# State-space taps of the second network's odd layer: shifted copies kept in DRAM, loads moved to GpSimd's queue, small products reordered

## The chip, the cores and the metric

The program runs on one core of one Trainium2 chip. The metric is the device time of one execution in microseconds (us), lower is better. Engines are named as in the profile: PE (TensorE matmul), PEld (TensorE weight load), DVE (VectorE), ACT (ScalarE), POOL (GpSimd), SP (SyncE, which here only issues transfers). All transfers, whoever issues them, are run by the core's 16 DMA engines.

## The reference

The program is a chain of two small networks on 256 tokens of width 2048. The part that matters here is the odd layer of the second network: a linear projection, a diagonal state-space model ("s5") on 128 groups of 16 channels, a gated linear unit, an output projection, and around it cross-attention to a memory and a squared-ReLU feed-forward layer.

```
def s5_mixer(u, lam_re, lam_im, log_dt, b_re, b_im, c_re, c_im, d_skip, w_glu, b_glu):
    ...
    lam_bar = jnp.exp(lam * dt)
    b_bar = ((lam_bar - 1.0) / lam)[..., None] * lax.complex(b_re.astype(f32), b_im.astype(f32))
    c_mat = lax.complex(c_re.astype(f32), c_im.astype(f32))
    ...
    def chunk_step(state, u_c):
        bu = jnp.einsum('bcgi,gpi->bcgp', u_c.astype(jnp.complex64), b_bar)
        bu = bu.at[:, 0].add(lam_bar * state)
        _, states = lax.associative_scan(combine, (a_elem, bu), axis=1)
        y = jnp.einsum('bcgp,gip->bcgi', states, c_mat).real
        return states[:, -1], y
    ...
    z = jax.nn.gelu(y)
    out = z * jax.nn.sigmoid(z @ w_glu.astype(f32) + b_glu.astype(f32))
    return out.astype(u.dtype)
```

## The kernel before

The kernel is written against a framework that takes the operations in program order, gives each engine's instructions an order by a timeline of its own, and adds the waits. A change in the program can therefore move instructions that it does not mention.

The dense layers read each weight tile (512 KB, tile `wraw`) on SP's queue, copy its high part on ACT (`wh`, L308), take the low part on DVE (`wl`, L309), and multiply both on PE. `dense_p` (L392, L393) holds the weight as the stationary operand, and `mm_t` (L344 to L346) and `mm_n` (L350 to L352) are two other forms. `wraw` has 3 buffers here, `wh` and `wl` 2 each and one more inside some stages.

The state-space layer is turned into products of small matrices, in 8 blocks of 16 groups, in two halves of the program.

The first half, `s5_gen` with `s5_block`, is a generator. It runs in the background of the first feed-forward layer (`ffn(0)`, about 1840 to 2600 us), a step at each tick. For each block it makes three tables and stores them in DRAM on ACT's queue (`store`, L269): `GD` (input to state, 1 MB per block), `HD` (state to output, 1 MB), and `KD` (the taps of the direct path). The taps come from 16 products `pk` (L1833, operands `bd` and `H`), 8 of them with the stationary operand in each half; each writes 32 of the 128 output columns of the array, and `o` picks which by `g % 4`. `KD` holds for each group and channel a row of 240 numbers: 112 zeros (`zpad`, written once) and 128 taps.

The second half, `odd`, runs after it (about 2600 to 3050 us):

- `v_gen` (L1888 on) loads `GD` as tile `gts`, multiplies it with the input `U` (L1898), transposes (L1905) and carries the states (`V`).
- beside it and behind it, `memkv` (L1606 on) makes keys and values of the memory from the weights `xattn_wkv` and the tile `mm`; its products are the L344 to L346 and L350 to L352 whose operand is `mhl`.
- then a loop over the 8 blocks, two at a time (`B`): DVE carries the states and copies them to one of two tiles `Xb` (L1976); the tile `tts` (1 MB) gets the taps, 8 shifted windows of `KD`, one transfer per shift (L1979); the tile `hts` gets `HD` (L1981); PE multiplies `U` with `tts` (L1986, 32 columns each) and `Xb` with `hts` (L1990, 64 columns each), both into `py`; ACT copies (`ys`, L1992), PE transposes (L1997), DVE adds (`zs`, L2001). Each two blocks give four tiles of the gated unit's input, and `glu_gen` steps through its weights (`s5_w_glu`, in the trace `s_w_glu`) in between.

`gts`, `tts` and `hts` share one tag with 3 buffers, so the load of a tile waits until the products of an earlier one have been issued and done. All these loads stand on SP's queue among the weight loads, in one order:

```
1978  for t in range(8):
1979      nc.sync.dma_start(tt[16 * t:16 * t + 16], KD[16 * blk:16 * blk + 16, :, 112 - 16 * t:240 - 16 * t].rearrange("g j x -> j g x"))
1981  nc.sync.dma_start(ht.rearrange("p a b c -> p (a b c)"), HD[blk])
```

A row of the first transfer is 128 numbers, 512 B, and one block has 2048 such rows; a row of the second is 2048 numbers, 8 KB.

POOL has little to do: among others it fills `zpad` and `Xb` with zeros, copies `pr`, and raises to the power of minus a half for the norms (`pow_mhalf`, L465), once near the start of `ffn(0)` and once in `odd`.

Of the kernel before, what the change touches and what calls it, by code (L numbers as in the profile page):

```python
# [10 lines left out]
F32 = mybir.dt.float32  # L11
# [11 lines left out]
HD = 128  # L23
# [190 lines left out]
class Prog:  # L214
# [1490 lines left out]
    def s5_gen(self, p, dr):  # L1705

        nc, a = self.nc, self.a
        GD, HD, KD = dr
        eng = nc.gpsimd
        f = lambda v: v.rearrange("p a b -> p (a b)")  # L1710
        lam = p.tile([128, 3, 64], F32, name="lam")
# [56 lines left out]
            nc.gpsimd.tensor_copy(pr[:, :, i], pw[:, :, 7 - i])  # L1768
        z = p.tile([128, 16, 112], F32, name="zpad", tag="G")
        nc.gpsimd.memset(z, 0.0)  # L1770
        self.store(KD[:, :, :112], z)
        yield
        for blk in range(8):
            yield from self.s5_block(p, dr, pw, pr, fb, blk)
# [5 lines left out]

    def s5_block(self, p, dr, pw, pr, fb, blk):
        nc, a = self.nc, self.a
        GD, HD, KD = dr
        keep = self.tc.keep_in_program_order
        gs = slice(blk * 8, blk * 8 + 8)
        bc = self.s5bc.pop(0)
# [34 lines left out]
        for i, (x, y, op) in enumerate(((0, 2, ALU.add), (2, 0, ALU.subtract))):  # L1821
            for g in range(0, 8, GS):
                c = slice(g, g + GS)
# [3 lines left out]
                yield  # L1827

        pk = self.sm((4, 128))
        for g in range(8):  # L1830
            o = pk[32 * (g % 4):32 * (g % 4) + 32, g // 4]
            for i in range(2):
                nc.tensor.matmul(o, bd[:, i, g].rearrange("p a b -> p (a b)"), H[:, i, g, :8].rearrange("p a b -> p (a b)"), start=i == 0, stop=i == 1)  # L1833
        self.store(HD[blk].rearrange("p (r g x) -> p r g x", r=2, g=8), H[:, :, :, 1:].rearrange("p r g t i -> p r g (t i)"))
        kc = p.tile([128, 2, 128], F32, name="kc", bufs=2)
        nc.scalar.copy(kc, pk[:, :2])
        for s in range(2):
            g0 = 16 * blk + 8 * s
            self.store(KD[g0:g0 + 8].rearrange("g j x -> (g j) x")[:, 112:], kc[:, s])
        yield  # L1840

        G = p.tile([128, 2, 8, 8, 16], F32, name="G", tag="G")
# [21 lines left out]
    def odd(self, x, uT, dr, kv, st, st_out):  # L1864

        nc, a = self.nc, self.a
        GD, HD, KD, UD = dr
        with self.pool("ohz") as hp, ExitStack() as es:
            up = es.enter_context(self.pool("ou"))
            U = up.tile([128, 128, 32], F32, name="U")  # L1870
# [16 lines left out]
            def v_gen():  # L1887

                for blk in range(8):
                    gt = sp.tile([128, 8, 2, 128], F32, name="gts", tag="st", bufs=3)  # L1890
                    nc.sync.dma_start(gt.rearrange("p a b c -> p (a b c)"), GD[blk])

                    pv = self.sm((2, 2, 128))
                    for g in range(8):
                        q = slice(32 * (g % 4), 32 * (g % 4) + 32)
                        for h in range(2):
                            hs = slice(64 * h, 64 * h + 64)
                            nc.tensor.matmul(pv[q, g // 4, :, hs], Ug(2 * (8 * blk + g) + h), gt[:, g, :, hs], start=True, stop=True)  # L1898
                    vs, ct = (lambda v: (v[:, 0], v[:, 1]))(up.tile([128, 8, 8, 16], F32, name="ys", bufs=2).rearrange("p (z i r) a b -> p z i r (a b)", z=2, i=2))
                    nc.scalar.copy(vs, pv)  # L1900
                    yield
                    tp = self.sm((2, 2, 4, 32))
                    for i in range(2):
                        for r in range(2):
                            nc.tensor.transpose(tp[:, r, i].rearrange("p a b -> p (a b)"), vs[:, i, r], self.cst("ident"))  # L1905
                    for r in range(2):
                        nc.scalar.copy(V[:, :, r, 8 * blk:8 * blk + 8], tp[:, r].rearrange("p i q c -> p c (i q)"))
                    carry(0, 1, 2, 16, L8, 8 * blk, ct.rearrange("p i r x -> p (i r x)"))
                    carry(1, 3, 4, 8, L16, 8 * blk, ct.rearrange("p i r x -> p (i r x)"))
                    yield  # L1910
# [54 lines left out]
            for B in range(4):  # L1965
                ys = up.tile([128, 8, 8, 16], F32, name="ys", bufs=2)
                for blk in (2 * B, 2 * B + 1):
# [7 lines left out]
                        for i in range(2):  # L1975
                            nc.vector.tensor_copy(xb[r, i, :, h, 1:], V[r, :31, i, gs].rearrange("p c g -> p g c"))  # L1976
                    tt = sp.tile([128, 16, 128], F32, name="tts", tag="st", bufs=3)
                    for t in range(8):
                        nc.sync.dma_start(tt[16 * t:16 * t + 16], KD[16 * blk:16 * blk + 16, :, 112 - 16 * t:240 - 16 * t].rearrange("g j x -> j g x"))  # L1979
                    ht = sp.tile([128, 2, 8, 128], F32, name="hts", tag="st", bufs=3)  # L1980
                    nc.sync.dma_start(ht.rearrange("p a b c -> p (a b c)"), HD[blk])  # L1981
                    py = self.sm((4, 128))
                    for b in range(4):
                        for q in range(4):
                            g = 4 * b + q
                            nc.tensor.matmul(py[32 * q:32 * q + 32, b], Ug(16 * blk + g), tt[:, g], start=b == 0, stop=False)  # L1986
                    for g in range(8):
                        o = py[64 * (g % 2):64 * (g % 2) + 64, g // 2]
                        for i in range(2):
                            nc.tensor.matmul(o, xb[:, i, g].rearrange("p a b -> p (a b)"), ht[:, i, g], start=False, stop=(i == 1 and g >= 6))  # L1990
                    b0 = 4 * (blk % 2)
                    nc.scalar.copy(ys[:, :, b0:b0 + 4], py.rearrange("p b (t i) -> p t b i", t=8))  # L1992
                zs = up.tile([128, 4, T], F32, name="zs", tag="zs", bufs=1)
# [89 lines left out]
    def second(self, xc, st):  # L2083
# [5 lines left out]
        GD = dp.tile([8, 128, 2048], F32, name="GD")  # L2089
        HD = dp.tile([8, 128, 2048], F32, name="HD")  # L2090
        KD = dp.tile([128, 16, 240], F32, name="KD")
        self.blocks = [dp.tile([128, 32, 32], F32, name=n) for n in ("MD", "XD", "YD")]
        UD = dp.tile([D, T], F32, name="UD")
        out = self.stat()
# [4 lines left out]
        with self.wide("w3"):  # L2099
            self.xattn(0, x, kv, st, s2)  # L2100
            st = self.stat()
            with self.pool("s5p") as p:
                self.bg.append(self.s5_gen(p, (GD, HD, KD)))
                self.ffn(0, x, s2, st, RF)
        s1 = self.stat()
        kv = (self.es.enter_context(self.pool("kv1")).tile([128, 4, T], F32, name="mkT"), kv[1])
        self.odd(x, xc[:, 0], (GD, HD, KD, UD), kv, st, s1)
        s2 = self.stat()
        s3 = self.stat()
        with self.wide("w4"):  # L2110
# [65 lines left out]
```

## Time and profile before

| | |
|---|---|
| three runs | 3854.62, 3855.39, 3858.6 us, median 3855.39 |
| the profiled execution | 3850.04 us, of which the span of instructions is 3848.3 us |
| PE busy | 3654.7 us (95%), at a mean granted clock of 0.975 |
| DVE, ACT, POOL busy | 2694.8 (70%), 1680.5 (44%), 102.1 us (3%) |
| DMA | 700.74 MB, 57.1% of 16 engines on SP's queue, 2.4% on ACT's, 0.4% on POOL's |

The profiled execution is 5.35 us below the median of the runs. A window of the profile gives for a stretch of the span how long each engine was busy, the granted PE clock as a share of full speed, and the DMA share (mean busy share of the 16 engines; packets in flight overlap, so it can pass 1). The chain view follows back from the last instruction what released it, step by step.

### The profile page before, as it was taken

What the parts mean: (1) busy time and instruction counts of PE and PEld (TensorE: products, weight loads), DVE (VectorE), ACT (ScalarE), POOL (GpSimd) and SP (SyncE); (2) the same over time, 40 slices, a digit from 0 to 9 for tenths busy, and PEclk for the clock granted to TensorE, in tenths of its full rate; (3) what the DMA queues carried; (4) which work ended last, traced back from release to release, by engine and by line L of the source; (5) the groups of instructions that cost most, each with busy time, mean ns of one, the idle gap of its engine ahead of it and who ended that gap; (6) DMA issues with size and microseconds to landing.
All of it is one profiled execution on the core that took longest, in us unless ns stands there. A gap on an engine that the chain in (4) does not pass through costs nothing.

```text
span 3848.3 us, 54892 instructions
## 1 busy us (share of the span) xinstructions
PE 3654.7 (95%) x21008; PEld 3029.0 (79%) x21008; DVE 2694.8 (70%) x4732; ACT 1680.5 (44%) x2524; POOL 102.1 (3%) x138
## 2 busy tenths in 40 slices
PE   6999999989999999899999999999879999999997
PEld 2677777777678889777888888887778788888886
DVE  3568777765776878767987778786666676656565
ACT  3313233262564566425544444444325454445353
POOL 0010000001000001000000000000000000000000
PEclk8999999999999999889999999999989999999999
DMA  9745544555655544524666666668985556666664
GB/s 343 244 145 176 158 149 156 175 170 174 215 152 158 142 137 140 164 67 145 188 214 197 208 200 208 198 211 247 223 197 181 165 154 191 187 191 187 190 186 148
DMA packets 609335, 700.74 MB, mean 182 GB/s; under 512 B 52208, under 2 KB 493680, under 8 KB 605744
## 3 DMA queue, kind: packets, MB, share of 16 engines
q1 hardware_dynamic: 576304, 662.39, 57.1%
q10 hardware_dynamic: 31488, 30.64, 2.4%
q0 software_dynamic: 1280, 4.20, 0.4%
q8 instruction: 165, 2.70, 0.3%
q14 instruction: 98, 0.80, 0.1%
HBM read 672.63 MB, written 24.51 MB: 181 GB/s over the span
## 4 chain that ended last, share of the span: by engine, by line
PE 82%; DMA 9%; DVE 6%; ACT 2%; issue 1%; SPq 0%; ACTq 0%; POOL 0%; DVEq 0%; POOLq 0%
PE acc L392 33%; PE acc L393 17%; PE acc L344 4%; PE acc L345 4%; PE acc L346 4%; PE acc L350 3%; PE acc L352 3%; PE acc L351 3%; DMA wraw<-ada_w 2%; DVE wl L309 2%; PE sm L623 1%; ACT wh L308 1%; PE sm L600 1%; DMA wraw<-w_in 1%; DMA tts<-KD 1%
## 5 line engine op out<-in xcount | busy, mean ns | idle before, releaser
L308 ACT CAST wh<-wraw 128x1024 fp32r<-128x1024 f32 x994 | 1037.7, 1045 | 1486.3 <-PE acc L392 734.1
L309 DVE TENSOR_TENSOR wl<-wraw,wh 128x1024 fp32r<-128x1024 f32 x994 | 1208.5, 1217 | 643.8 <-ACT wh L308 639.6
L392 PE MATMUL acc<-hl,wh 128*128 128x512 f32 x3008 | 1060.4, 400 | 21.9 <-DVE hl L490 15.1
L393 PE MATMUL acc<-hl,wl 128*128 128x256 f32 x3008 | 827.3, 284 | 4.3 <-DVE wl L309 4.3
L392 PE MATMUL acc<-hid,wh 128*128 128x512 f32 x2048 | 709.9, 394 | 1.4 <-DVE xc L526 1.0
L392 PEld LDWEIGHTS acc<-hl,wh 128*128 128x128 f32 x3008 | 559.3, 190 | 150.4 <-DVE hl L490 11.6
L393 PEld LDWEIGHTS acc<-hl,wl 128*128 128x128 f32 x3008 | 567.9, 190 | 23.4 <-DVE wl L309 8.1
L393 PE MATMUL acc<-hid,wl 128*128 128x256 f32 x2048 | 559.8, 280 | 0.0
L392 PEld LDWEIGHTS acc<-hid,wh 128*128 128x128 f32 x2048 | 378.3, 188 | 85.6 <-issue 1.8
L393 PEld LDWEIGHTS acc<-hid,wl 128*128 128x128 f32 x2048 | 380.9, 188 | 9.0 <-issue 3.4
L571 DVE SCALAR_TENSOR_TENSOR ada_a<-wraw,sc,ada_a 128x512 f32<-128x512 f32 x360 | 253.5, 749 | 19.6 <-DMA wraw<-ada_w 18.7
L344 PE MATMUL acc<-hl,wh 128*128 128x512 f32 (+2 forms) x688 | 256.0, 376 | 7.7 <-ACT wh L308 3.8
L345 PE MATMUL acc<-hl,wh 128*128 128x512 f32 (+2 forms) x688 | 252.9, 369 | 0.0
L346 PE MATMUL acc<-hl,wl 128*128 128x512 f32 (+2 forms) x688 | 247.1, 369 | 0.0
L350 PE MATMUL acc<-wh,hl 128*128 128x512 f32 (+1 forms) x504 | 200.1, 402 | 4.0 <-ACT wh L308 2.5
L351 PE MATMUL acc<-wh,hl 128*128 128x512 f32 (+1 forms) x504 | 199.7, 396 | 0.0
L352 PE MATMUL acc<-wl,hl 128*128 128x512 f32 (+1 forms) x504 | 189.2, 395 | 4.4 <-DVE wl L309 4.4
L526 DVE TENSOR_TENSOR xc<-acc,xc 128x256 f32<-128x256 f32 x384 | 141.8, 419 | 36.7 <-PE acc L393 36.1
L344 PEld LDWEIGHTS acc<-hl,wh 128*128 128x128 f32 (+1 forms) x688 | 130.2, 190 | 37.3 <-issue 6.6
L345 PEld LDWEIGHTS acc<-hl,wh 128*128 128x128 f32 (+1 forms) x688 | 130.0, 189 | 25.2 <-issue 5.9
L346 PEld LDWEIGHTS acc<-hl,wl 128*128 128x128 f32 (+1 forms) x688 | 129.1, 189 | 23.9 <-issue 3.2
L406 ACT COPY joined<-acc 128x256 f32<-128x256 f32 x188 | 69.5, 371 | 133.1 <-PE acc L393 133.0
(588 smaller groups left out, 4950.0 us busy)
## 6 DMA issues: line engine op xcount, KB each, us to landing
wraw<-ffn_up SPq DMA_DIRECT2D x256, 512.0 KB, 3.8
wraw<-ffn_down SPq DMA_DIRECT2D x256, 512.0 KB, 3.7
wraw<-ada_w SPq DMA_DIRECT2D x192, 512.0 KB, 4.5
wraw<-w_in SPq DMA_DIRECT2D x144, 512.0 KB, 4.4
wraw<-w_out SPq DMA_DIRECT2D x64, 512.0 KB, 4.5
wraw<-even_w_in SPq DMA_DIRECT2D x54, 512.0 KB, 3.7
wraw<-even_w_out SPq DMA_DIRECT2D x32, 512.0 KB, 3.6
wraw<-xattn_wkv SPq DMA_DIRECT2D x32, 512.0 KB, 4.7
```

Of the source, the lines that this page charges most:

```text
L308: nc.scalar.copy(hi, src)
L309: self.held(nc.vector.tensor_tensor(lo, src, hi.bitcast(F32), op=ALU.subtract))
L344: nc.tensor.matmul(A, h, xh, start=(start and first), stop=False)
L345: nc.tensor.matmul(A, h, xl, start=False, stop=False)
L346: nc.tensor.matmul(A, lo, xh, start=False, stop=(stop and last))
L350: nc.tensor.matmul(A, xh, wh[:, kk, :cw], start=start, stop=False)
L351: nc.tensor.matmul(A, xl, wh[:, kk, :cw], start=False, stop=False)
L352: nc.tensor.matmul(A, xh, wl[:, kk, :cw], start=False, stop=stop)
L392: nc.tensor.matmul(A, wh[:, kk, cs], xp, start=k == 0, stop=False)
L393: nc.tensor.matmul(A[:, 1], wl[:, kk, cs], xp[:, 0], start=False, stop=k == nk - 1)
L526: nc.vector.tensor_tensor(x[:, j + i], A[:, h], x[:, j + i], op=ALU.add)
L571: nc.vector.scalar_tensor_tensor(a[:, r], w[:, kk], c, a[:, r], op0=ALU.mult, op1=ALU.add)
```

## The change

`s5_block` now writes, as soon as a block's taps are in `KD`, the 8 shifted windows to a new array `TD` in DRAM, in the layout that `tts` has in SBUF. `odd` then loads `tts` in one transfer of 128 rows of 8 KB. The stores to `KD` (`zpad`, `kc`), the writes of `TD` (64 in all) and the loads of `gts`, `tts` and `hts` are issued by POOL. The loops over the small products `pk` and `Xb` x `hts` run in another order: four (two) groups with the first of their two terms, then the same groups with the second.

```
@@ s5_gen
-        self.store(KD[:, :, :112], z)
+        nc.gpsimd.dma_start(KD[:, :, :112], z)
@@ s5_block
-        for g in range(8):
-            o = pk[32 * (g % 4):32 * (g % 4) + 32, g // 4]
-            for i in range(2):
+        for g, i in ((4 * s + q, i) for s in range(2) for i in range(2) for q in range(4)):
+                o = pk[32 * (g % 4):32 * (g % 4) + 32, g // 4]
                 nc.tensor.matmul(o, bd[:, i, g].rearrange("p a b -> p (a b)"), H[:, i, g, :8].rearrange("p a b -> p (a b)"), start=i == 0, stop=i == 1)
...
-            self.store(KD[g0:g0 + 8].rearrange("g j x -> (g j) x")[:, 112:], kc[:, s])
+            nc.gpsimd.dma_start(KD[g0:g0 + 8].rearrange("g j x -> (g j) x")[:, 112:], kc[:, s])
+
+        for t in range(8):
+            nc.gpsimd.dma_start(TD[blk, 16 * t:16 * t + 16], KD[16 * blk:16 * blk + 16, :, 112 - 16 * t:240 - 16 * t].rearrange("g j x -> j g x"))
@@ odd
-                    nc.sync.dma_start(gt.rearrange("p a b c -> p (a b c)"), GD[blk])
+                    nc.gpsimd.dma_start(gt.rearrange("p a b c -> p (a b c)"), GD[blk])
...
-                    for t in range(8):
-                        nc.sync.dma_start(tt[16 * t:16 * t + 16], KD[16 * blk:16 * blk + 16, :, 112 - 16 * t:240 - 16 * t].rearrange("g j x -> j g x"))
+                    nc.gpsimd.dma_start(tt.rearrange("p g x -> p (g x)"), TD[blk].rearrange("p g x -> p (g x)"))
...
-                    nc.sync.dma_start(ht.rearrange("p a b c -> p (a b c)"), HD[blk])
+                    nc.gpsimd.dma_start(ht.rearrange("p a b c -> p (a b c)"), HD[blk])
...
-                    for g in range(8):
+                    for g, i in ((2 * r + h, i) for r in range(4) for i in range(2) for h in range(2)):
                         o = py[64 * (g % 2):64 * (g % 2) + 64, g // 2]
-                        for i in range(2):
-                            nc.tensor.matmul(o, xb[:, i, g].rearrange("p a b -> p (a b)"), ht[:, i, g], start=False, stop=(i == 1 and g >= 6))
+                        nc.tensor.matmul(o, xb[:, i, g].rearrange("p a b -> p (a b)"), ht[:, i, g], start=False, stop=(i == 1 and g >= 6))
@@ second
+        TD = dp.tile([8, 128, 16, 128], F32, name="TD")
```

**POOL's order.** From the zeros of `zpad` in the feed-forward layer to the loads of `odd`, before:

```order
L1770 MEMSET zpad 128x1792
L1768 COPY pr<-pw 128x2x64
L465 TENSOR_TENSOR rstd_c<-rstd_c,consts 128x2
L1768 COPY pr<-pw 128x2x64 x7
L1874 MEMSET Xb_22745 128x1024
L1874 MEMSET Xb_22746 128x1024
L465 TENSOR_TENSOR rstd_c<-rstd_c,consts 128x2 x4
```

and with the change, from the eighth block's stores to the first loads of `tts` and `hts` (a transfer of `zpad` stands between the first two rows above, and seven more pairs like the first two rows here stand ahead of these):

```order
L1838 DMA KD<-kc 128x128 x2
L1841 DMA TD<-KD 256x1x128 x8
L1876 MEMSET Xb_22810 128x1024
L1876 MEMSET Xb_22811 128x1024
L1893 DMA gts<-GD 128x2048 x3
L465 TENSOR_TENSOR rstd_c<-rstd_c,consts 128x2
L1893 DMA gts<-GD 128x2048 x5
L1980 DMA tts<-TD 128x2048
L1982 DMA hts<-HD 128x2048
```

All transfers of the state-space tables but the stores of `GD` and `HD` now follow one another on POOL, with two of its small jobs (the power for the feed-forward layer's norm and that for `odd`'s) behind some of them.

**SP's order.** Among the weight loads of `memkv`, where before

```order
L1981 DMA hts<-HD 128x2048
L314 DMA wraw<-xattn_wkv 128x2x512
L1979 DMA tts<-KD 16x16x128 x2
L1606 DMA mm<-memT 128x2x256
L1979 DMA tts<-KD 16x16x128 x6
L314 DMA wraw<-xattn_wkv 128x2x512
L1981 DMA hts<-HD 128x2048
L1979 DMA tts<-KD 16x16x128 x2
```

stood in SP's queue, with the change there are only weights and the memory, up to the gated unit's:

```order
L1606 DMA mm<-memT 128x2x256
L314 DMA wraw<-xattn_wkv 128x2x512 x2
L1606 DMA mm<-memT 128x2x256
L314 DMA wraw<-xattn_wkv 128x2x512 x3
L314 DMA wraw<-s_w_glu 128x2x512 x16
L314 DMA wraw<-s_w_glu 128x4x256 x16
```

SP loses 80 transfers and keeps the rest in nearly the same order.

**PE's order** in the feed-forward layer, around a block's first run of `pk` products (`sm<-H,bd` is a `pk` product, the dense rows are L392 and L393), before:

```order
L393 MATMUL acc<-hid,wl 128x256
L1833 MATMUL sm<-H,bd 32x128
L392 MATMUL acc<-hid,wh 128x512 x2
L1833 MATMUL sm<-H,bd 32x128 x6
L393 MATMUL acc<-hid,wl 128x256 x2
```

and with the change:

```order
L393 MATMUL acc<-hid,wl 128x256
L1832 MATMUL sm<-H,bd 32x128
L392 MATMUL acc<-hid,wh 128x512 x2
L1832 MATMUL sm<-H,bd 32x128 x3
L1859 MATMUL sm<-consts,G 128x128 x3
L393 MATMUL acc<-hid,wl 128x256 x2
```

The scheduler cuts the 128 `pk` products into 36 runs between dense products before, and into 30 with the change, and a run now holds more different groups.

## Rows read from the trace of the kernel before

**Rows 1.** The page's chain that ended last, by engine and by line.

```profile
PE 82%; DMA 9%; DVE 6%; ACT 2%; issue 1%; SPq 0%; ACTq 0%; POOL 0%; DVEq 0%; POOLq 0%
```

**Rows 2.** Windows: stretch, length, busy PE, PEld, DVE, ACT, POOL, then PEclk, DMA share, GB/s.

```profile
1860.00:2590.00 730.00, 728.60 (x4319) 622.30 (x4318) 584.78 (x954) 333.36 (x420) 4.61 (x7) 1.00 0.66 204
2724.00:2785.00 61.00, 49.22 (x384) 43.07 (x382) 33.59 (x85) 21.11 (x36) 0.00 (x0) 0.89 1.02 221
2785.00:2801.00 16.00, 9.88 (x47) 7.95 (x46) 15.28 (x49) 5.16 (x6) 0.00 (x0) 0.83 0.53 165
2801.00:2821.00 20.00, 12.36 (x169) 11.12 (x169) 19.81 (x88) 4.93 (x6) 0.00 (x0) 0.76 0.88 166
2821.00:2872.00 51.00, 43.34 (x471) 39.71 (x472) 22.87 (x49) 14.65 (x16) 0.00 (x0) 0.90 1.14 236
2872.00:2896.00 24.00, 23.38 (x199) 22.65 (x198) 10.50 (x15) 8.79 (x9) 0.00 (x0) 0.95 0.40 125
```

**Rows 3.** The chain from 2724 to 2896 us: start, length, what.

```profile
2728.32 9.80 DMA wraw<-xattn_wkv
...
2751.36 6.11 DMA tts<-KD
```

**Rows 4.** PE's waits from 2724 to 2896 us: total, times, longest.

```profile
PE sm L1990 <- DVE Xb L1976: 6.1, 1, 6.1
PE sm L1986 <- DMA tts<-KD: 6.1, 1, 6.1
...
PE sm L1990 <- DMA hts<-HD: 4.6, 3, 3.4
```

**Rows 5.** DMA, 2800 to 2880 us: tenths busy and rate per 2 us, issues.

```profile
DMA  1047999999999999999999999999999999996006
GB/s 60 8 66 291 267 122 122 123 157 389 163 128 140 166 244 329 139 146 150 191 365 413 389 153 142 166 189 340 381 284 137 167 182 246 389 406 236 2 0 162
...
hts<-HD SPq DMA_DIRECT2D x6, 1024.0 KB, 9.3
tts<-KD SPq DMA_DIRECT2D x40, 128.0 KB, 10.0
```

**Rows 6.** DMA, 2724 to 2800 us: issues, size, median to landing.

```profile
tts<-KD SPq DMA_DIRECT2D x24, 128.0 KB, 6.5
```

**Rows 7.** Timeline of SP at 2813 us: start, length, what.

```profile
2812.86 9.65 SPq L1979 DMA_DIRECT2D tts<-KD  x8
```

**Rows 8.** Timeline of PE: runs of `pk` records (two per product).

```profile
1952.28 0.66 PE L1833 MATMUL sm<-H,bd 128*32 128x128 f32 x16
...
1963.18 0.41 PE L1833 MATMUL sm<-H,bd 128*32 128x128 f32 x2
...
2018.50 0.63 PE L1833 MATMUL sm<-H,bd 128*32 128x128 f32 x6
...
2527.64 1.06 PE L1833 MATMUL sm<-H,bd 128*32 128x128 f32 x20
```

**Rows 9.** Line L1833: idle time of its engine, total and times.

```profile
  issue: 10.1, 31
```

**Rows 10.** All transfers: issues, KB each, median us to landing.

```profile
HD<-H ACTq DMA_DIRECT2D x8, 1024.0 KB, 7.4
...
x<-xc POOLq DMA_DIRECT2D x16, 256.0 KB, 3.6
```

**Rows 11.** Line L946, POOL's transfers before: ns min, median, max.

```profile
L946 POOL DMA_DIRECT2D x<-xc x16: 724/724/903, 622.4 to 764.7; - x16
```

**Rows 12.** Line L314 (weight loads) from 1956 to 1966 us.

```profile
DMA to landing us min/median/max: 4.0/5.1/5.2
```

**Rows 13.** PE's waits from 1840 to 2600 us, the one on weights.

```profile
PE acc L392 <- ACT wh L308: 0.4, 1, 0.4
```

**Rows 14.** Timeline of POOL, start of the feed-forward layer.

```profile
1837.65 1.59 POOL L1770 MEMSET zpad<- 128x1792 f32 x1 [53.04 <-DVE xc L526]
...
1856.05 0.70 POOL L465 TENSOR_TENSOR rstd_c<-rstd_c,consts 128x2 f32<-128x2 f32 x1 [16.34 <-DVE rstd_c L482]
```

More of the change, by code (lines that the diff above doesn't have):

```diff
@@ L1707, in s5_gen @@
         nc, a = self.nc, self.a
-        GD, HD, KD = dr
+        GD, HD, KD, TD = dr
         eng = nc.gpsimd
@@ L1782, in s5_block @@
         nc, a = self.nc, self.a
-        GD, HD, KD = dr
+        GD, HD, KD, TD = dr
         keep = self.tc.keep_in_program_order
@@ L1866, in odd @@
         nc, a = self.nc, self.a
-        GD, HD, KD, UD = dr
+        GD, HD, _, TD, UD = dr
         with self.pool("ohz") as hp, ExitStack() as es:
@@ L2102, in second @@
             with self.pool("s5p") as p:
-                self.bg.append(self.s5_gen(p, (GD, HD, KD)))
+                self.bg.append(self.s5_gen(p, (GD, HD, KD, TD)))
                 self.ffn(0, x, s2, st, RF)
@@ L2106, in second @@
         kv = (self.es.enter_context(self.pool("kv1")).tile([128, 4, T], F32, name="mkT"), kv[1])
-        self.odd(x, xc[:, 0], (GD, HD, KD, UD), kv, st, s1)
+        self.odd(x, xc[:, 0], (GD, HD, KD, TD, UD), kv, st, s1)
         s2 = self.stat()
```

## The prediction, made before the changed kernel ran

> **What bounds the kernel now.** I read the chain first: 82% of it is PE, and 9% is DMA [rows 1], so somewhere transfers set the pace. The windows say where [rows 2]. In the feed-forward layer (1860 to 2590) PE is busy 728.60 of 730 us at a granted clock of 1.00: that is PE alone, with a DMA share of 0.66. In 2724 to 2785 and in 2821 to 2872 PE is busy 49.22 of 61 and 43.34 of 51 us, and the DMA share is 1.02 and 1.14: DMA alone. In between (2785 to 2821) DVE is busy 15.28 of 16 and 19.81 of 20 us: there the states are carried, and nothing else counts. The chain agrees: in the first DMA stretch it goes over weights and `tts` [rows 3], and PE's longest waits there and behind are on `tts`, on `Xb` (DVE) and on `hts` [rows 4].
>
> What makes DMA the bound is not the bytes. Per 2 us, the same 16 engines move 122 to 170 GB/s while mostly `tts` is under way, and 329 to 413 while `hts` or weights are [rows 5]. The first has 512 B rows, the others several KB. One `tts` (1.05 MB) at about 135 GB/s costs 7.8 us of all engines' time, at about 385 GB/s 2.7. The difference, **5.1 us per block**, is the core of this forecast (an estimate from that row).
>
> **The change, part by part.**
>
> *First DMA stretch, 2724 to 2785.* 24 issues of `tts` [rows 6], that is 3 blocks, each 5.1 us cheaper: 15.3 us less DMA time. What can be won: PE is idle for 61 - 49.2 = 11.8 us, and at a granted clock of 0.89, part of the time at 1.2 GHz instead of 2.4, it loses 0.11 x 61 = 6.7 us; together 18.5. What is left afterwards: DMA work of 1.02 x 61 - 15.3 = 47 us, PE work of 42.5 us, two near equals that never overlap wholly. So between 6 and 15, and I take **-11**.
>
> *DVE's stretch, 2785 to 2821.* DVE does the same work. **0**, at best -3, since a DMA share of 0.88 in its second part leaves little waiting behind it.
>
> *Second DMA stretch and its tail, 2821 to 2896.* 5 blocks (40 issues [rows 5]) save 25.5 us of about 68 (1.14 x 51 + 0.40 x 24). That is more than can be used: PE is idle 7.7 + 0.6 = 8.3 us, and its clock (0.90, 0.95) costs 5.1 + 1.2 = 6.3, so 14.6 is the ceiling; from there PE is the bound. One thing stays: `gts`, `tts` and `hts` still share three buffers, so an `hts` starts when a slot frees, and waits on `hts` (4.6 in all now [rows 4]) need not all go. Between 5 and 14; I take **-10**.
>
> *SP's queue.* SP loses 80 issues. 8 shifts held it for 9.65 us [rows 7], during which no weight behind them could start. This lies in the same two stretches, so it is not counted again; it is one more reason for their gains.
>
> *`pk` in the feed-forward layer.* This is on the path, since PE has no idle time there. The page's runs give the price [rows 8]; a product is two records. One product takes 0.41 us; 8 products on four column groups, two on each, 0.66; 3 products of which two or more share a column group, 0.63; 10 products, 1.06. So time goes with the most products that one column group gets in a run (a "round"), at (1.06 - 0.41) / 3 = 0.215 us each from one round to four. Counted over all runs in PE's order, the rounds sum to 63 before and to 41 with the change, because a cut run now holds different groups: 22 x 0.215 = 4.7 us. The runs fall from 36 to 30, and each costs an issue gap of 10.1 / 31 = 0.33 us [rows 9]: 2.0 us. Together **-6.7**; 0 if the scheduler's surroundings give it back, -10 if the dense products behind the runs start sooner too.
>
> The Trainium skill speaks against this count ("TensorE: Matmul & The Clock Gate", Part 3): matmuls start and end strictly in program order. By it, pairs of one group written side by side would hold up the next groups, a run of 8 would need 5 rounds before and 2 now, and the reordering would be worth more: 8 blocks x 3 x 0.215 = 5.2 us in whole runs alone. The run of 8 in the old order says two rounds, so the trace does not agree, and the page changes no term here.
>
> That run, 0.66 us with neighbours side by side [rows 8], shows that a product of another group starts past one that has to wait. So the reordering of `Xb` x `hts`, whose two column groups are full in either order, is costed at nothing.
>
> *`TD` writes.* New work in the feed-forward layer: 64 transfers of 128 KB, eight bursts of 1 MB in 512 B rows, DRAM to DRAM. No row shows DRAM to DRAM. The nearest is the store of `HD`, 1 MB, 7.4 us to landing [rows 10]; beside one of these a weight lands in 5.1 us [rows 12], and PE's waits on weights in the whole layer sum to 0.4 us [rows 13]. How late may a weight be? 204 GB/s over 730 us is 149 MB, 284 loads of 512 KB, one per 2.6 us; with three buffers a load has under 7.8 us, of which the copies on ACT and DVE take some. Seen without a wait: 5.2. I put the limit at 6 (an estimate between the two). If a burst is like an `HD` store, it costs nothing; if it holds weights 4 us beyond the limit each time, 8 x 4 = 32 (that end is rival 3's ground). I take **+2**, near the row.
>
> *POOL.* Costed at nothing, because POOL is idle there (4.61 us of 730 busy [rows 2]). A load issued by it takes 0.72 us [rows 11], so 24 loads take 17 us over 300. The store of `zpad`, 2048 rows against 128 in that row, is at most 16 x 0.72 = 11.6 us, ahead of the power for the norm, which comes 16.8 us after the zeros end [rows 14]. Were that cover gone, PE would wait for the norm once, a few us. ACT loses 17 issues; it is not the bound anywhere here.
>
> *Sum* against the profiled execution: 3850.0 - 11 - 0 - 10 - 6.7 + 2 = 3824.3, that is -25.7. That execution is 5.35 us below the runs' median of 3855.39; on the median, where I put the forecast, **3830**.
>
> **The rivals.**
>
> 1. *POOL's queue is the slow one.* A 256 KB load issued by POOL lands in 3.6 us [rows 10]; if that scales with size, 1 MB takes 14 us against 9.3 for `hts` on SP [rows 5]. Three buffers then give one table per 5 us, while 16 of them are used in some 150 us, but unevenly: the first stretch gains only 3, the second 5, and DVE's stretch loses about 8 because PE stands before `hts` when `Xb` is ready. With -4.7 for `pk`: -5, **3850**, no change that can be told. For it: the only POOL rows are small. Against it: 3.6 us for 256 KB is mostly fixed time, as `hts` shows (four times the bytes in 2.6 times the time, on busier engines).
>
> 2. *The rows are not the reason.* If `tts` takes 7.8 us in long rows too, the DMA time of both stretches is unchanged. Only the waits on `hts` behind eight issues go (4.6), and `pk` gives 4.7: **3846**. Against it stands the row of rates [rows 5]. The Trainium skill ("DMA: Bandwidth & Descriptors", Specifications) would side with this rival: it states that 512 B is already enough for line rate. The trace disagrees: 122 to 170 GB/s at 512 B.
>
> 3. *Slower: the `TD` bursts starve PE.* DRAM to DRAM reads and writes the same memory, and the read rows here step through `KD` at 960 B. If a burst makes weights land later than the limit of 6 us, every us beyond it is on the path, eight times, in a layer without slack. The gain of 27.7 is eaten at 3.5 us per burst; beyond 4.4 us the kernel is slower than can be mistaken for noise. At 8 us per burst (the engines twice as long as for an `HD` store): +64 - 28, some **3890**; at 6, 3875. For it: a DMA share of 0.66 in the layer means that a burst of 8 us takes as much of the engines as they have free in 24 us, and the `HD` store comes close to it in time. Against it: each burst is spread over eight issues on one queue behind the weights' own, and the store of `HD` shows no harm.
>
> **How the numbers follow.** A measurement of this kernel can tell about 0.2%, 7.7 us, from no change. The forecast has 0.70, rival 1 0.12, rival 2 0.08, rival 3 0.10. The forecast's own terms reach, not all at their ends together, from -40 to -13 us: 3816 to 3842. Rival 2 lies at 3846 and rival 1 at 3850, so the range goes to 3852 and leaves out rival 3 and the forecast's tails. Faster: 0.70 + 0.08 = 0.78; same: 0.12; slower: 0.10.
>
> **What would show it.** Right: `tts` is one load of 1 MB that lands in about 6 us; in the two DMA stretches the rate is above 300 GB/s with a share under 1, PE's wait on `tts` is gone, and they are shorter by 11 and 10; the next wait is on `hts` or, in DVE's stretch, still on `Xb`. In the feed-forward layer there are about 30 runs of `pk`, none of 3 or 4 products over 0.45 us, and the layer is 5 to 7 us shorter. Wrong: weights there that land later than 6 us beside `TD` and a PE wait on `wh` of several us in each block (rival 3); `hts` or `gts` landing in 12 us or more, or POOL transfers that take over 2 us to issue (rival 1); `tts` still at 8 us or more with the engines to itself (rival 2). A layer that is no shorter although the runs are would mean that my count of rounds prices nothing.

## The result, and the profile after

The changed kernel takes 3811.61 us (median of 4 runs, 3809.28 to 3816.4) against 3855.42 before in the same comparison: a ratio of 0.9892, 95% interval 0.988 to 0.9904. It is faster, as forecast, but by 43.8 us where 25 were forecast, and it lies under the range (3816 to 3852).

To compare stretches I cut both traces at the same six dense products of PE; in the kernel before these start at 1860.39, 2600.13, 2724.11, 2785.41, 2821.12 and 2896.07 us, close to the cuts of [rows 2]. Lengths in us by the profiled executions, with the second profiles of both kernels that are told of below:

| stretch | before | again | after | again | change | forecast |
|---|---|---|---|---|---|---|
| feed-forward layer | 739.74 | 739.75 | 734.06 | 733.42 | -5.7 | -4.7 |
| `U` and the `gts` products | 123.98 | 127.90 | 121.44 | 122.97 | -2.5 | 0 |
| first DMA stretch | 61.30 | 62.25 | 49.28 | 48.65 | -12.0 | -11 |
| DVE's stretch | 35.71 | 35.24 | 29.28 | 29.29 | -6.4 | 0 |
| second DMA stretch and tail | 74.95 | 75.35 | 64.45 | 64.92 | -10.5 | -10 |
| sum | 1035.7 | 1040.5 | 998.5 | 999.3 | -37.2 | -25.7 |

The other 6.6 of the 43.8 us are not found in these stretches. They come with the executions that were profiled: the one of before was 5.4 us under its median, the one of after (3813.57) 2 over it. What lies ahead of the layer is the same code in both kernels and took from 1854.5 to 1866.0 us over all profiles of this study, so a few us between the whole times of two profiles say nothing.

The last three stretches of the kernel before, cut like this (columns as in [rows 2]; each product of PE is at least one record, counted behind the x):

```profile
2724.11:2785.41 61.30, 49.45 (x383) 42.96 (x381) 33.89 (x86) 21.41 (x36) 0.00 (x0) 0.89 1.02 219
2785.41:2821.12 35.71, 22.01 (x214) 19.19 (x214) 34.80 (x137) 9.68 (x12) 0.00 (x0) 0.79 0.73 167
2821.12:2896.07 74.95, 66.67 (x669) 62.31 (x668) 33.30 (x63) 23.43 (x25) 0.00 (x0) 0.92 0.90 201
```

All five stretches of the changed kernel:

```profile
1860.21:2594.27 734.06, 731.95 (x4377) 627.00 (x4376) 590.08 (x962) 337.05 (x426) 49.16 (x87) 1.00 0.70 217
2594.27:2715.71 121.44, 113.57 (x759) 93.02 (x758) 80.64 (x157) 53.08 (x86) 6.92 (x12) 0.97 0.86 250
2715.71:2764.99 49.28, 45.76 (x383) 40.03 (x382) 36.11 (x94) 21.78 (x36) 2.59 (x5) 0.97 0.88 275
2764.99:2794.27 29.28, 19.01 (x215) 16.53 (x213) 28.86 (x112) 9.45 (x12) 2.63 (x5) 0.88 0.68 232
2794.27:2858.72 64.45, 63.83 (x669) 59.54 (x668) 37.47 (x80) 23.63 (x25) 3.23 (x6) 0.97 0.64 220
```

DMA no longer fills either of the two DMA stretches: the share fell from 1.02 to 0.88 and, over the second with its tail, from 0.90 to 0.64, and there PE is busy 63.83 of 64.45 us. The chain says the same. Before, its pieces of `wraw`, `tts` and `hts` transfers from 2724 to 2896 us sum to 72.8 us; after, from 2715 to 2859 us, it has none. Over the whole kernel its DMA share fell from 9% [rows 1] to 7% (8% in a second profile):

```profile
PE 82%; DVE 7%; DMA 7%; ACT 2%; issue 1%; SPq 0%; ACTq 0%; POOL 0%; DVEq 0%; POOLq 0%
```

DMA from 2770 to 2850 us, to be held against [rows 5]: there are gaps now, `tts` is one transfer, and while `tts` and `hts` move without a pause (2784 to 2796 us) the rate is 324 to 410 GB/s. Over the whole stretches it is 275 and 220 (the windows above).

```profile
DMA  6266407989989637407759989999866778135071
GB/s 164 100 190 184 158 0 197 410 332 328 401 369 324 233 82 291 201 5 260 230 119 393 318 238 395 410 397 413 283 222 161 175 328 326 62 51 220 0 235 37
...
hts<-HD POOLq DMA_DIRECT2D x6, 1024.0 KB, 6.2
tts<-TD POOLq DMA_DIRECT2D x5, 1024.0 KB, 7.4
```

PE's waits from 2715 to 2859 us, against [rows 4]: 6.1 on `tts` became 2.0, 4.6 on `hts` became 1.1, and the 6.1 on `Xb` (DVE) stands at 4.9.

```profile
PE sm L1990 <- DVE Xb L1978: 4.9, 1, 4.9
PE sm L1987 <- DMA tts<-TD: 2.0, 1, 2.0
PE sm L1990 <- DMA hts<-HD: 1.1, 1, 1.1
```

In the feed-forward layer, `pk` in the listing by line, first before, then after (busy, mean ns, idle before):

```profile
L1833 PE MATMUL sm<-H,bd 128*32 128x128 f32 x256 | 20.7, 280 | 0.0
L1833 PEld LDWEIGHTS sm<-H,bd 128*32 128x32 f32 x256 | 11.1, 108 | 11.7 <-issue 10.1 <-PE acc L393 0.7 <-DVE H L1826 0.6
```

```profile
L1832 PE MATMUL sm<-H,bd 128*32 128x128 f32 x256 | 14.9, 281 | 0.0
L1832 PEld LDWEIGHTS sm<-H,bd 128*32 128x32 f32 x256 | 6.9, 108 | 9.9 <-issue 7.5 <-PE acc L393 0.7 <-DVE wl L309 0.6
```

PE spends 5.8 us less on them and 2.6 us less in issue gaps, 8.4 in sum; the layer is shorter by 5.7, so some of it is given back elsewhere in the layer. No run of 3 or 4 products takes more than 0.43 us now. The run of 0.63 us in [rows 8], three products of which two share a column group, is now one of two products in two groups (the x counts records, two per product):

```profile
2018.49 0.41 PE L1832 MATMUL sm<-H,bd 128*32 128x128 f32 x4
```

Beside `TD`'s bursts the slowest weight of the layer lands in 9.1 us instead of 7.4, and PE waits 1.1 us on `wh` in all, against 0.4 [rows 13].

### The profile page after: what moved, and what is told of

Its sections match the earlier page's. It is cut to its first block, busy times and chain, and to the rows that moved or that the text cites. A ratio compares the mean times of both kernels' runs of the same rounds, so it can differ in the third digit from the quotient of the medians.

```text
span 3811.8 us, 54931 instructions
## 1 busy us (share of the span) xinstructions
PE 3636.8 (95%) x21008; PEld 3016.5 (79%) x21008; DVE 2695.3 (71%) x4732; ACT 1679.9 (44%) x2524; POOL 160.8 (4%) x243
## 4 chain that ended last, share of the span: by engine, by line
PE 82%; DVE 7%; DMA 7%; ACT 2%; issue 1%; SPq 0%; ACTq 0%; POOL 0%; DVEq 0%; POOLq 0%
PE acc L392 34%; PE acc L393 17%; PE acc L344 4%; PE acc L346 4%; PE acc L345 4%; PE acc L350 3%; PE acc L352 3%; PE acc L351 3%; DMA wraw<-ada_w 2%; DVE wl L309 2%; PE sm L623 1%; DMA wraw<-w_in 1%; PE sm L600 1%; ACT wh L308 1%; DMA xc<-xc 1%
## 5 line engine op out<-in xcount | busy, mean ns | idle before, releaser
L392 PE MATMUL acc<-hl,wh 128*128 128x512 f32 x3008 | 1060.8, 400 | 22.3 <-DVE hl L490 15.2
L393 PE MATMUL acc<-hl,wl 128*128 128x256 f32 x3008 | 827.5, 284 | 3.5 <-DVE wl L309 3.5
L392 PE MATMUL acc<-hid,wh 128*128 128x512 f32 x2048 | 709.6, 394 | 2.1 <-ACT wh L308 1.1
L392 PEld LDWEIGHTS acc<-hl,wh 128*128 128x128 f32 x3008 | 559.7, 190 | 149.8 <-DVE hl L490 11.7
L393 PEld LDWEIGHTS acc<-hl,wl 128*128 128x128 f32 x3008 | 568.8, 190 | 22.8 <-DVE wl L309 6.8
L393 PE MATMUL acc<-hid,wl 128*128 128x256 f32 x2048 | 559.2, 280 | 0.0
L392 PEld LDWEIGHTS acc<-hid,wh 128*128 128x128 f32 x2048 | 378.3, 188 | 86.4 <-issue 2.2
L393 PEld LDWEIGHTS acc<-hid,wl 128*128 128x128 f32 x2048 | 381.0, 188 | 8.7 <-issue 2.8
```

The costliest lines, as they stand in the source:

```text
L392: nc.tensor.matmul(A, wh[:, kk, cs], xp, start=k == 0, stop=False)
L393: nc.tensor.matmul(A[:, 1], wl[:, kk, cs], xp[:, 0], start=False, stop=k == nk - 1)
```

## The experiments

### What the order of the small products is worth

`order_only` is the kernel before with this alone (and the same for `Xb` x `hts`), `old_order` the changed kernel without it (the products' own lines are left out here):

```
-        for g in range(8):
-            for i in range(2):
+        for g, i in ((4 * s + q, i) for s in range(2) for i in range(2) for q in range(4)):
```

> The kernel before with the two loops over small products in the new order and nothing else. Rounds theory (time of a run goes with the most products of one column group): the feed-forward layer 740.0 us, from 1860 to 2600, becomes 733 to 735 us, the state-space stretches 2600 to 2896 (296 us) stay within 2 us; in all 5 to 7 us faster than before. Rival (the order prices nothing, the layer got shorter for another reason, such as queues freed on ACT): the layer stays at 739 to 741 us and the time within 2 us.

> The changed kernel with the two loops over small products back in the old order. Rounds theory: 5 to 7 us slower than the changed kernel, all of it in the feed-forward layer (734.3 us becomes 739 to 741). Rival (the order prices nothing): within 2 us of it.

Measured, `order_only`: 0.9969 of before (0.9957 to 0.9982), the layer 736.47 us, 3.3 less, where 5 to 7 were expected. `old_order`: 0.9933 (0.9921 to 0.9946), the layer 741.47 us, 7.4 more than after (6 to 8 against its three profiles). So the order is worth 3 to 8 us there, and nothing in the state-space stretches (`old_order`: DVE's 28.88, the last 64.75 us). The spread goes along with the cuts that the scheduler makes: 31 runs of `pk` in `order_only`, 30 after, 38 in `old_order`, and the `pk` products with their issue gaps take 7.2 us less than before in the one and 10.6 more than after in the other. By the medians the two kernels differ by more than their layers, 12.7 us from before and 17.0 from the changed kernel beside it. The profiles do not show that surplus in any stretch that the order touches, and it stays unexplained.

### Rows, width or number of transfers

Four kernels before with only the load of `tts` altered, all on SP, with no `TD`. The taps' part of the output is missing in all four, since they load other data of the same size in place of the taps:

```
long_rows_1   nc.sync.dma_start(tt.rearrange("p g x -> p (g x)"), HD[blk])
long_rows_8   for t in range(8): nc.sync.dma_start(tt[16 * t:16 * t + 16].rearrange("p g x -> p (g x)"), HD[blk, 16 * t:16 * t + 16])
wide_512      nc.sync.dma_start(tt, KD[:, :, 112 - 16 * blk:240 - 16 * blk])
wide_8        for t in range(8): nc.sync.dma_start(tt[:, 2 * t:2 * t + 2].rearrange("p g x -> p (g x)"), HD[blk][:, 256 * t:256 * t + 256])
```

> The kernel before, but each block's tts is loaded from HD (same size, 128 rows of 8 KB) by one transfer on SP, so the taps' part of the output is left out and there is no TD and no work on POOL. Row theory: tts lands in 5 to 7 us, and the stretches 2724 to 2785, 2785 to 2821 and 2821 to 2896 (61, 36 and 75 us) become about 47, 31 and 64, as in the changed kernel; 26 to 30 us faster in all, layer unchanged. Queue theory (what helped is that POOL issues the loads and SP only weights): at most 5 to 8 us faster, since the loads still stand among the weights on SP.

> As long_rows_1, but in 8 transfers of 16 rows of 8 KB on SP, as many issues as in the kernel before (the taps' part of the output is left out). Row theory: within 4 us of long_rows_1, so 22 to 30 us faster than before. Issue theory (what cost was that 8 issues hold SP's queue for 9.65 us and spread over all its rings): within 5 us of the kernel before.

> The kernel before, with tts loaded by one transfer on SP that goes to all 128 partitions, 16 rows of 512 B each, from the same array KD (a group's row per partition, so the taps' part of the output is left out). Row theory of the prediction (512 B rows cost 5.1 us per block): tts takes 8 us or more, stretches near 61, 36 and 75 us, within 6 us of the kernel before. Partition theory (a transfer into 16 partitions is slow, whatever its rows) and issue theory (8 transfers are): like long_rows_1, 45, 32 and 59 us, 25 to 33 us faster than before.

> The kernel before, with tts loaded from HD in 8 transfers on SP as before, each now to all 128 partitions in rows of 1 KB (the taps' part of the output is left out). Partition theory: near long_rows_1, stretches about 46, 33 and 61 us, 22 us faster than before or more. Issue theory (8 issues in SP's queue): near long_rows_8, 57, 32 and 73 us, about 10 us faster. Row theory: between the two, as 1 KB lies between 512 B and 8 KB.

| `tts` by | partitions of one transfer | rows | three stretches, us | sum | ratio to before |
|---|---|---|---|---|---|
| 8 transfers (before) | 16 | 512 B | 61.30, 35.71, 74.95 | 172.0 | 1 |
| 8 (`long_rows_8`) | 16 | 8 KB | 57.55, 32.08, 72.62 | 162.3 | 0.9973 (0.9962 to 0.9984) |
| 8 (`wide_8`) | 128 | 1 KB | 50.93, 30.20, 67.45 | 148.6 | 0.9941 (0.9924 to 0.9958) |
| 1 (`wide_512`) | 128 | 512 B | 51.72, 32.06, 59.49 | 143.3 | 0.9937 (0.9921 to 0.9953) |
| 1 (`long_rows_1`) | 128 | 8 KB | 45.48, 32.52, 59.29 | 137.3 | 0.9915 (0.99 to 0.9931) |

Rows 16 times as long, with the rest kept, save 9.7 us in 16 partitions and 6.0 in 128. Going from 16 partitions to 128 with as many transfers saves 13.7, although the rows get shorter; going from eight transfers to one 5.3 more, again with shorter rows (this last step is from the profiles alone, the two ratios do not tell it). So the prediction's reason, row length, is the smaller part. The sums are what to compare: in `wide_512` and `long_rows_1` the middle stretch holds 32 more records of PE than in the kernel before (x246 and x247 against x214), and the last about as many fewer. The rates show the cause directly. DMA of `long_rows_8` from 2810 to 2840, `tts` in 8 KB rows into 16 partitions, with `hts` and weights between:

```profile
DMA  8998999969999999999998999999999889999699
GB/s 131 175 153 131 175 153 153 175 240 437 415 350 131 142 142 153 153 153 186 153 175 306 371 426 317 131 175 175 164 175 186 137 134 199 300 385 344 158 347 311
```

and of `wide_512` from 2780 to 2820, where `tts` comes in the old 512 B rows out of `KD`, but into all partitions (the last third):

```profile
GB/s 127 350 16 8 137 348 76 283 205 63 342 119 25 291 209 82 342 117 0 0 0 131 254 393 335 336 306 305 397 434 326 317 289 292 382 418 311 129 313 326
```

131 to 175 GB/s against 289 to 336 (the slices in which only such rows move): the width of the transfer decides, and 512 B rows by themselves run at over twice what [rows 5] seemed to say of them. The Trainium skill ("SBUF — State Buffer", Door 1: The DMA port swizzle) has the rule: a transfer's bandwidth depends on how many of the 16 ports its partitions reach, and 16 neighbours reach 4 of them; at 27 GB/s a port (435 over 16) that is 109 GB/s, an estimate from that page. The trace agrees in kind, with 131 to 175. That it shows more than the estimate would fit with two shifts under way on different ports, which no run here separates.

The windows of `long_rows_1`, in whose first and last stretch PE is busy nearly all the time:

```profile
2720.96:2766.44 45.48, 44.32 (x383) 38.82 (x382) 36.05 (x94) 21.86 (x36) 0.00 (x0) 1.00 0.89 295
2766.44:2798.96 32.52, 22.74 (x247) 20.05 (x245) 32.24 (x126) 9.73 (x13) 0.00 (x0) 0.81 0.71 240
2798.96:2858.25 59.29, 59.29 (x636) 56.80 (x636) 33.44 (x66) 23.12 (x25) 0.00 (x0) 0.99 0.65 224
```

### Whose queue

`short_rows_pool` is the kernel before with the loads of `gts`, `tts` and `hts` as they were, but issued by POOL (`nc.sync` becomes `nc.gpsimd` in three places); `after_loads_sp` is the changed kernel with these three back on SP.

> The kernel before with the loads of gts, tts (8 transfers of 512 B rows from KD) and hts issued by POOL; SP issues only weights. Row theory: the engines have the same work, tts still takes 7 to 10 us, and the three stretches stay within 6 us of 61, 36 and 75; 0 to 8 us faster in all. Queue theory: 25 us faster or more, as in the changed kernel.

> The changed kernel with the loads of gts, tts and hts back on SP's queue, tts still one transfer of 8 KB rows from TD. Row theory: within 6 us of the changed kernel, so 30 us or more faster than before. Queue theory: 15 us or more slower than the changed kernel, since loads that wait for a free buffer hold up the weights behind them on SP.

`short_rows_pool`: 1.0018 (1.0007 to 1.0029), no faster than before, with 61.68, 33.08 and 87.85 us (windows below), 10.6 more in sum. The last stretch got 12.9 longer, also since 32 records of PE moved into it from the middle one; `tts` lands in 10.3 us in the median and PE's waits on it come to 10.6.

```profile
2724.46:2786.14 61.68, 49.28 (x383) 42.01 (x381) 33.47 (x82) 21.09 (x35) 14.51 (x26) 0.89 1.04 210
2786.14:2819.22 33.08, 19.29 (x181) 16.25 (x182) 30.77 (x121) 10.29 (x12) 8.28 (x14) 0.85 0.64 157
2819.22:2907.07 87.85, 70.93 (x701) 66.67 (x700) 38.19 (x83) 23.61 (x25) 18.93 (x33) 0.86 0.84 186
```

`after_loads_sp`: 0.9881 (0.9863 to 0.9899) against 0.9892 of the changed kernel, with 46.82, 30.72 and 61.23 us, 138.8 in sum against 143.0. So POOL's queue brings nothing; it is only no worse, once the transfers are wide.

### What `TD` costs

```
td_one_block   if blk == 0: for t in range(8): (TD written), and TD[0] read by all blocks
td_twice       the same eight transfers once more, to TD2, which nobody reads
```

> The changed kernel with TD written for the first block only, 8 transfers of 64, and read from there by all eight blocks (so seven blocks use the taps of the first). If the TD bursts cost nothing in the layer, as an HD store does: within 1.5 us of the changed kernel. By the term of the prediction (2 us for eight bursts): 1 to 2 us faster. If they hold up weights: 7 bursts of 1 us or more, 7 us faster or more.

> The changed kernel with every TD transfer written twice, the second time to an array that nobody reads: eight more bursts of 1 MB in 512 B rows. If a burst is wholly hidden and has room left: within 2 us of the changed kernel. If weights then land past PE's need: 8 x 1 to 4 us, 8 to 32 us slower, with PE waiting on wh in each block.

`td_one_block`: 0.9905 (0.9891 to 0.9918), its layer 736.34 us, no shorter than with all 64 writes (734.06, 733.42 and, in a third profile, 735.55); it leaves PE's wait on `wh` at 1.0. `td_twice`: 0.9918 (0.9906 to 0.9931), its layer 741.28, 6 to 8 longer, of which PE's waits on weights are 4.7 + 0.5, in four places and not in each block:

```profile
PE acc L392 <- ACT wh L308: 4.7, 3, 3.7
...
PE acc L393 <- DVE wl L309: 0.5, 1, 0.5
```

So eight bursts cost nothing that shows, and the room ends with the next eight. The layers have to tell this: by its median `td_one_block` is 6.2 us slower than the changed kernel beside it, with less to do.

### Why DVE's stretch got shorter

The stretch is full of DVE work in both kernels (34.80 of 35.71 us, 28.86 of 29.28), so I had costed it at nothing. But PE waits for a transfer inside it. In the kernel before, PE's first `Xb` product starts 15.4 us into the stretch, and the wait on `tts` of [rows 4] lies behind it:

```profile
2800.78 6.36 PE L1990 MATMUL sm<-hts,Xb 128*64 128x128 f32 x64 [6.05 <-DVE Xb L1976]
2818.88 1.94 PE L1986 MATMUL sm<-tts,U 128*32 128x128 f32 x32 [6.05 <-DMA tts<-KD]
```

In the changed kernel the first starts 12.5 us into it (at 2777.50), 2.9 sooner, and the wait on `tts` is 2.0, 4.1 less; the other pieces give 0.5 back. That is the 6.4. The chain agrees: before, it went over these two transfers almost wholly inside the stretch, and after it does not.

```profile
2807.17 4.30 DMA tts<-KD
2811.53 10.66 DMA hts<-HD
```

Four runs look at DVE's share. `xb_on_act` moves the 32 copies to `Xb` to ACT in the changed kernel; `wl_on_pool` lets POOL make the low parts of `xattn_wkv` in the kernel before; `sp_wl_pool` and `sp_wl_half` do the latter for 16 and for 8 tiles in `after_loads_sp`.

```
xb_on_act    nc.vector.tensor_copy(xb[...], ...)       -> nc.scalar.copy(xb[...], ...)
wl_on_pool   nc.vector.tensor_tensor(lo, src, hi, ...) -> nc.gpsimd, for the weights of the second memkv
```

> The changed kernel with the 32 copies to Xb done by ACT instead of DVE (they cost DVE 6.4 us of the 31.3 us in which it is always busy). If DVE bounds that stretch in the changed kernel: it falls by 3 to 6 us, to 25 to 28 us, and the kernel is that much faster. If ACT's copies of weights then come late, or hts bounds the stretch: within 2 us of the changed kernel, or slower.

> The kernel before, with the low parts of the second memory's weights (wl of xattn_wkv, 16 tiles) made by POOL instead of DVE, so that DVE's state steps no longer stand behind a subtraction that waits for a late weight. Backlog theory: DVE has no or one state step left where PE begins the stretch of 35.7 us (3 in the kernel before), Xb is ready 3 us or more earlier in it, and it falls to 31 to 33 us although the stretch ahead of it stays at 59 to 63. Rival (that stretch got shorter in the changed kernel only by its own transfers): it stays at 34 to 36.

> The changed kernel with its loads on SP (after_loads_sp) and with wl of xattn_wkv (16 tiles) made by POOL, whose queue then holds none of those loads. Backlog theory: with DMA no longer the bound ahead of it, the gain in the DVE stretch is kept: the two stretches 46.8 and 30.7 us (77.5 in sum) become 70 or less, 7 us or more faster than the changed kernel. Rival (POOL's 2.4 us per tile, twice DVE's, makes the weights late as in wl_on_pool): the first grows by as much as the second falls, within 3 us of the changed kernel.

> As sp_wl_pool, with every second wl of xattn_wkv (8 tiles) on POOL and the others on DVE. Backlog theory: between 70 and 77.5 us for the two stretches, near sp_wl_pool if POOL is the slower one there; 4 us or more faster than the changed kernel. Rival: within 3 us of it.

`xb_on_act`: 0.9884 (0.9866 to 0.9903), the stretch 30.85 us; no gain. DVE is busy only 27.49 us then, but ACT is busy 21.19 us where it was 9.45.

`wl_on_pool`: 0.9985 (0.9974 to 0.9997). Its first two stretches:

```profile
2718.36:2790.35 71.99, 54.17 (x416) 46.06 (x414) 57.39 (x136) 21.65 (x36) 31.06 (x13) 0.86 0.93 198
2790.35:2813.11 22.76, 18.66 (x216) 15.84 (x214) 22.62 (x67) 9.99 (x12) 4.75 (x2) 0.95 1.00 241
```

DVE's stretch falls from 35.71 to 22.76, the one ahead grows by 10.7, where 31 to 33 and no growth were expected. Some products of PE moved ahead of the cut (x416 against x383), so the two belong together: 94.8 us against 97.0. What tells of a backlog is when DVE makes the first copy to `Xb`. Counted from the first cut, that is 75.6 us before, 60.9 in `wl_on_pool` (at 2779.24) and 60.7 in the changed kernel (before, then after):

```profile
2799.70 1.29 DVE L1976 COPY Xb<-V 64x248 f32<-64x248 f32 x4
```

```profile
2776.42 1.30 DVE L1978 COPY Xb<-V 64x248 f32<-64x248 f32 x4
```

So the state work could be done nearly 15 us earlier while the loads of `tts` were as slow as before: a part of it is a backlog. The run does not separate DVE's waits for weights from the time of the 16 subtractions themselves. The waits are seen in DVE's timeline of the kernel before, at the edge of the stretch, where state steps (L1956 to L1960) stand behind subtractions `wl` in DVE's order:

```profile
2779.10 0.29 DVE L1958 TENSOR_TENSOR sc_tmp<-L,V 128x128 f32<-128x128 f32 x1
2784.13 1.23 DVE L309 TENSOR_TENSOR wl<-wraw,wh 128x1024 fp32r<-128x1024 f32 x1 [4.75 <-ACT wh L308]
2785.28 0.28 DVE L1959 TENSOR_TENSOR sc_tmp<-sc_tmp 128x128 f32<-128x128 f32 x1
```

The step is cut in two, with 4.75 us of idle time and the late weight between its halves. DVE's waits in the first DMA stretch, before and after:

```profile
DVE wl L309 <- ACT wh L308: 26.3, 9, 7.9
```

```profile
DVE wl L309 <- ACT wh L308: 11.3, 7, 4.8
```

That is 15 us less standing. Of the 5.9 us that DVE is busy less in its stretch, 2.2 moved into the stretch ahead (33.89 to 36.11). Another 4.2 went into the one behind (33.30 to 37.47): state steps of later blocks and one low part `hl`, which in the kernel before stand ahead of the cut. So a part of the work in its stretch was not needed there.

With the transfers wide, more of the backlog can't be had cheaply that way: `sp_wl_pool`, 0.9933 (0.992 to 0.9946), has 64.30 and 22.48 us there (POOL takes 2.4 to 2.5 us for a tile where DVE takes 1.2), `sp_wl_half`, 0.9917 (0.9904 to 0.9929), 49.38 and 26.97, against 46.82 and 30.72 of `after_loads_sp`: 86.8 and 76.4 in sum against 77.5. Neither beats the changed kernel beside it (0.9906).

### The same kernels again

> The kernel before once more, for a second profile: which stretch differs between its executions, given that the profiled one was 5.35 us under the median. If the spread lies where DMA bounds (2724 to 2785, 2821 to 2896), these differ by 3 us or more and the layer by less than 1; if it lies elsewhere (the early stages up to 1100 us), the state-space stretches repeat within 1.5 us.

> The changed kernel once more, as the anchor for the runs beside it and as a second profile. Both theories: 0.988 to 0.990 of the kernel before; stretches within 1.5 us of 734.3, 121.5, 47.3, 31.3 and 64.4 us. If these differ by more, the 7 us between the gain by the profiled executions (36.5 us) and by the medians (43.8 us) lie in that stretch.

> The changed kernel beside these two on the same chip, as their anchor: 0.988 to 0.990 of the kernel before, stretches within 1 us of 49, 29.3 and 64.7 us.

`before_again` took 3848.52 us; its second stretch is 3.9 us longer than in the first profile, the others repeat within 1 us (table above), and its layer began 5.1 us earlier. `after_again`: 0.9889 (0.9874 to 0.9905); `after_third`: 0.9906 (0.9894 to 0.9919), with 735.55 in the layer. Over all profiles the code ahead of the layer scatters by 11 us and the code behind the last cut, which no run changed, takes from 949.9 to 959.0. So a median can move by several us through stretches that the change does not touch.

## Why the prediction was wrong

Two steps failed: the price of DVE's stretch, which is the largest miss (6.4 of the 11.5 us between the forecast's terms, -25.7, and the profiles, -37.2), and the reason for the core term, which does not show in the time.

- **DVE's stretch, "0, at best -3"**: failed, -6.4 by the first profiles. "DVE does the same work", and "nothing else counts" there, took a full engine for the bound. PE's wait of 6.1 us on `tts`, which the prediction had read in [rows 4], lies in this very stretch, at 2812.8 to 2818.9, and became 2.0. DVE's part of it was partly late work, put off by DVE's order behind subtractions that waited for weights: PE's first `Xb` product came 2.9 us sooner. A DMA share of 0.88 there was taken to mean little waiting; the chain went over a `tts` and an `hts` transfer for 15 us just there.
- **Reason for 5.1 us per block**: wrong. "The first has 512 B rows, the others several KB" tied the rate to the rows; what differed as well in [rows 5] was that each `tts` transfer fills 16 partitions and an `hts` 128. That the size was nearly right is luck: the change mends both. The long-row, one-transfer kernel saves 34.7 us over three stretches, wide 512 B rows 28.7 of these.
- **What bounds, first and second DMA stretch**: -12.0 and -10.5 against -11 and -10. Right, with PE as the next bound in the last one. Two of the signs did not come: the rate over the stretches is 275 and 220 GB/s, not above 300, and PE's wait on `tts` shrank to 2.0 but is not gone.
- **`U` and `gts`**: costed at nothing, -2.5 by the first profiles. By the second profiles it is -4.9, and this stretch moves by 4 us between executions of the same kernel, so its size stays open.
- **`pk`**: -6.7 forecast; the `pk` rows themselves show -8.4, the layer 3.3 and 7.4 in two settings. Right in kind, and in size within what the layer gives back. `Xb` x `hts`: nothing, right.
- **`TD`**: +2 forecast, no cost that shows; at double the writes 6 to 8. Rival 3 was wrong by its price: beside a burst the slowest weight came 1.7 us later (0.8 later in `td_one_block`, away from its one burst), not 4 to 8. The limit of 6 us for a weight was also too low: weights landed in up to 7.4 us before and 9.1 after, with waits of PE of 0.4 and 1.1 us in all.
- **POOL**: costed at nothing, right with wide transfers. Rival 1 falls: `hts` lands in 5.6 us from POOL, 8.1 before. **Rival 2** was right in its premise, that the rows were not the main reason, and wrong in its conclusion that `tts` would stay slow. The page of the Trainium skill that I set against the trace there ("DMA: Bandwidth & Descriptors", Specifications) comes closer to the runs than I did: 512 B rows run at 289 to 336 GB/s when the transfer is wide. It is not the whole of it, since 8 KB rows still save 6.0 us there.
- **The range** ended at 3816, 4.4 us short. It allowed no gain beyond 3 us in a stretch that I had called another engine's, and none in `U` and `gts`. It also carried the 5.35 us between one profiled execution and the median over as if it were fixed; after the change it was 2 us the other way, and these 7 us alone would have put the result inside. So scatter had a hand in the miss as well.

## What to carry to other kernels

Before blaming the rows of a slow load, look how many partitions one transfer fills, and compare it with a wide transfer in the same rows: here the width and the number of transfers together were worth 25 to 29 us and the row length 6 to 10. An engine that is busy throughout a stretch is not its bound until one has seen that its work could not have been done earlier or later: look for its waits in the stretch ahead, and for waits of PE on anything else inside the stretch. Moving loads to another queue gained nothing here.

## What was not expected of the hardware

Eight narrow transfers per block are no better from POOL: 182.6 us over the three stretches where SP's took 172.0. And transfers into 16 partitions ran at nearly the same rate whatever their rows, 131 to 175 GB/s with 8 KB and 122 to 170 with 512 B, while the DMA engines were busy eight or nine tenths of the time and more: a full share does not mean that no more bytes could be moved.
